# Half of the gate and up rows of two feed-forward layers by seven block products for eight, with the sums of weight tiles made by accumulating DMAs

## The chip, the cores and the metric

The program runs on one core of one Trainium2 chip. The metric is the device time of one execution in microseconds (us). Engines are named as the profile names them: PE multiplies matrices, PEld loads its stationary operands, DVE and ACT do elementwise work, POOL is the fourth engine and can issue DMAs, SP issues DMAs. PSUM holds the results of PE in eight banks of 128 x 512 numbers.

## What is computed

A decoder trunk of two layers on 256 tokens of 2048 features, in float32: a state-space layer (S5) with a gated output, then an attention layer, each followed by the same feed-forward part. Only that part is touched:

```python
def rmsnorm(x, g):
    xf = x.astype(jnp.float32)
    y = xf * lax.rsqrt(jnp.mean(xf * xf, axis=-1, keepdims=True) + EPS)
    return (y * g.astype(jnp.float32)).astype(x.dtype)

def swiglu(u, w_gate, w_up, w_down):
    return (jax.nn.silu(u @ w_gate) * (u @ w_up)) @ w_down
...
        u = rmsnorm(h, g_ffn[i])
        h = h + swiglu(u, w_gate[i], w_up[i], w_down[i])
```

Here u is 256 x 2048, w_gate and w_up are 2048 x 5632, w_down is 5632 x 2048.

## The kernel before

Every weight matrix is cut on the host into tiles of 512 rows by 512 columns, 1 MB each, and 344 such tiles pass through one stream of **jobs** (`jobs`, `add`). A job loads its tile into a raw buffer (`load_upto`, SP's queue, a ring of three), splits it into a high and a low part in two halves of 1024 elements a partition (`split_upto`: `hi` by ACT on line 98, `lo` = raw - hi by DVE on line 99), and multiplies (`mm3`, lines 108 to 110): for each of four row blocks of 128 and each half of the tokens three products of 128 x 128 by 128 x 512, high by high, low by high and high by low, so 24 matmuls a job. The activations stand split in the same way (`uT`, from `hT_blocks`, lines 141 to 146).

The gate and up work of a layer is cut into 11 **chunks** of 512 columns, chunks 0 to 5 and then 6 to 10, each part followed by its share of the down products. A chunk is eight jobs: gate with row groups 0 to 3, then up with row groups 0 to 3. Behind them come `gate_evac` (Silu, line 686, ACT), `up_evac` (times up, line 693, DVE) and `g_rows` (for each token half four transposes on PE, line 701, the high part on ACT, line 704, the low part on DVE, line 705).

The order is written out by hand. `run_stream` emits for job i: its own split if that isn't done, its matmuls, the split of job i+1, and then the functions hung on job i (`after`, filled from `pend`). Every engine takes its instructions in this order. So an evacuation that hangs on job i stands on ACT and DVE behind the split of job i+1 and ahead of the split of job i+2, which is wanted when job i+2 starts. `hi` and `lo` are two buffers each; the split of a job needs the buffers of the job two before it.

```python
            j.mm(j)
            split_upto(i + 2)
            for f in j.after:
                f()
```

## Time and profile before

| | us |
|---|---|
| median of 3 runs (2116.31 to 2117.63) | 2116.36 |
| profiled execution, its own time | 2113.61 |
| its span, first to last instruction | 2111.8 |
| PE busy | 2082.5 (99%) |
| DVE busy | 1135.2 (54%) |
| ACT busy | 905.6 (43%) |
| POOL busy | 150.1 (7%) |

The sums are made against the profiled execution: 2113.61, of which 1.8 us lie around the span. A busy share is an average over the whole program, so the stretch that is changed has to be looked at by itself. The granted clock of PE is 0.998 of full speed over the span.

### The profile page before, as it was taken

To read this page: it belongs to the slowest core of one execution; us is meant where nothing else is said; L and a number is where in the kernel's file an instruction comes from. 1 tells how busy PE (TensorE), PEld (TensorE's weight loads), DVE (VectorE), ACT (ScalarE), POOL (GpSimd) and SP (SyncE) were. 2 spreads that over 40 slices of the span, in tenths; PEclk is the share of its full clock that TensorE was granted. 3 is DMA by queue.
4 is the path that set the end of the run, shared out by engine and by line. 5 is a ranking of instruction groups with operands and counts; after the bars stand their busy time and mean duration, and the time that the engine had idled before them with its cause. 6 is when DMAs were issued, how large, how long until landed. Compare 5 with 4: busy or idle time off the path is not lost.

```text
span 2111.8 us, 27975 instructions
## 1 busy us (share of the span) xinstructions
PE 2082.5 (99%) x11712; PEld 1754.9 (83%) x11712; DVE 1135.2 (54%) x1661; ACT 905.6 (43%) x1161; POOL 150.1 (7%) x105
## 2 busy tenths in 40 slices
...
GB/s 140 25 126 157 197 190 188 197 183 197 182 197 199 181 197 180 198 180 180 180 160 180 172 167 160 181 193 184 185 194 193 186 199 190 189 192 186 195 194 149
DMA packets 54046, 376.14 MB, mean 178 GB/s; under 512 B 6432, under 2 KB 6944, under 8 KB 9120
## 3 DMA queue, kind: packets, MB, share of 16 engines
...
q14 instruction: 35, 0.29, 0.0%
...
## 4 chain that ended last, share of the span: by engine, by line
PE 95%; DVE 3%; ACT 1%; issue 1%; DMA 0%; SPq 0%; ACTq 0%; POOLq 0%; POOL 0%
PE acc L109 18%; PE acc L110 18%; PE acc L108 18%; PE x L110 4%; PE x L108 4%; PE x L109 4%; PE tr L109 4%; PE tr L108 4%; PE tr L110 4%; PE acc L793 3%; PE acc L792 3%; PE acc L791 3%; PE x L464 1%; PE tr L141 1%; PE acc L273 1%
## 5 line engine op out<-in xcount | busy, mean ns | idle before, releaser
L99 DVE TENSOR_TENSOR lo<-raw,hi 128x1024 fp32r<-128x1024 f32 x674 | 805.9, 1237 | 674.5 <-ACT hi L98 674.4
L98 ACT ACTIVATE hi<-raw 128x1024 fp32r<-128x1024 f32 x688 | 690.4, 1052 | 715.4 <-PE acc L109 413.3
L108 PE MATMUL acc<-hi,g 128*128 128x512 f32 x704 | 274.9, 390 | 0.0
L110 PE MATMUL acc<-lo,g 128*128 128x512 f32 x704 | 274.0, 389 | 0.0
L109 PE MATMUL acc<-hi,g 128*128 128x512 f32 x704 | 274.0, 389 | 0.0
L108 PE MATMUL acc<-hi,u_f 128*128 128x512 f32 x640 | 251.1, 392 | 1.1 <-ACT hi L98 1.0
L110 PE MATMUL acc<-lo,u_f 128*128 128x512 f32 x640 | 249.5, 390 | 1.1 <-DVE lo L99 1.1
L109 PE MATMUL acc<-hi,u_f 128*128 128x512 f32 x640 | 249.3, 390 | 0.0
L110 PEld LDWEIGHTS acc<-lo,g 128*128 128x128 f32 x704 | 132.2, 188 | 27.6
L109 PEld LDWEIGHTS acc<-hi,g 128*128 128x128 f32 x704 | 132.2, 188 | 27.1
L108 PEld LDWEIGHTS acc<-hi,g 128*128 128x128 f32 x704 | 132.2, 188 | 27.1
L108 PE MATMUL x<-hi,u_f 128*128 128x512 f32 x384 | 151.3, 394 | 0.0
L110 PE MATMUL x<-lo,u_f 128*128 128x512 f32 x384 | 149.7, 390 | 0.0
L109 PE MATMUL x<-hi,u_f 128*128 128x512 f32 x384 | 149.5, 389 | 0.0
L108 PE MATMUL tr<-hi,u_f 128*128 128x512 f32 x384 | 149.4, 389 | 0.0
L109 PE MATMUL tr<-hi,u_f 128*128 128x512 f32 x384 | 149.4, 389 | 0.0
L110 PE MATMUL tr<-lo,u_f 128*128 128x512 f32 x384 | 149.4, 389 | 0.0
L110 PEld LDWEIGHTS acc<-lo,u_f 128*128 128x128 f32 x640 | 120.1, 188 | 26.9 <-DVE lo L99 1.9
L108 PEld LDWEIGHTS acc<-hi,u_f 128*128 128x128 f32 x640 | 120.2, 188 | 26.4 <-ACT hi L98 1.9
L109 PEld LDWEIGHTS acc<-hi,u_f 128*128 128x128 f32 x640 | 120.2, 188 | 24.8 <-DVE u_f L146 0.3
L110 PEld LDWEIGHTS x<-lo,u_f 128*128 128x128 f32 x384 | 72.1, 188 | 15.2
L108 PEld LDWEIGHTS tr<-hi,u_f 128*128 128x128 f32 x384 | 72.1, 188 | 15.0
...
## 6 DMA issues: line engine op xcount, KB each, us to landing
raw<-w_gate SPq DMA_DIRECT2D x88, 1024.0 KB, 4.8
raw<-w_up SPq DMA_DIRECT2D x88, 1024.0 KB, 4.8
raw<-w_down SPq DMA_DIRECT2D x88, 1024.0 KB, 4.8
raw<-w_kv SPq DMA_DIRECT2D x32, 1024.0 KB, 4.8
raw<-w_glu SPq DMA_DIRECT2D x16, 1024.0 KB, 4.9
raw<-w_q SPq DMA_DIRECT2D x16, 1024.0 KB, 4.8
raw<-w_o SPq DMA_DIRECT2D x16, 1024.0 KB, 4.8
h<-x_tok SPq DMA_DIRECT2D x2, 1024.0 KB, 7.8
```

The costliest lines, as they stand in the source:

```text
L98: act.activation(j.hi[:, s], j.raw[:, s], AF.Copy)
L99: (pool if i < NPRE else dve).tensor_tensor(j.lo[:, s], j.raw[:, s], j.hi[:, s], op=OP.subtract)
L108: pe.matmul(pr, oh, j.hi[:, kb], start=first and kb == 0, stop=False)
L109: pe.matmul(pr, ol, j.hi[:, kb], start=False, stop=False)
L110: pe.matmul(pr, oh, j.lo[:, kb], start=False, stop=last and kb == 3)
L141: pe.transpose(tr[:, bb, a], h[:, a, 128 * b:128 * b + 128], ident)
L273: pe.matmul(wbk[:, 0:w], ident, cs[:, 0:w], start=True, stop=True)
L464: pe.matmul(yb[64 * g2:64 * g2 + 64, g], H[q][r, ri, gl + g2].rearrange("p k c -> p (k c)"), Z[r, :, ri, 2 * (8 * o + g) + b], start=ri == ...
L791: pe.matmul(p, j.hi[:, kb, s], u[:, 0], start=first and kb == 0 and n % 2 == 0, stop=False)
L792: pe.matmul(p, j.hi[:, kb, s], u[:, 1], start=False, stop=False)
L793: pe.matmul(p, j.lo[:, kb, s], u[:, 0], start=False, stop=last and kb == 3 and n % 2 == 1)
```

## The change

In both layers chunk 0 stays as it was in its products. In the other ten chunks of a layer, row groups 2 and 3 stay (four jobs of 24 matmuls), and row groups 0 and 1 are computed together for gate and up by Strassen's method: the activations are a 2 x 2 block matrix (two token halves by two row groups), the weights are one too (two row groups by gate and up), and seven products of blocks stand for eight. Each of the seven is a job of 12 matmuls (`mm1`). Three of them use blocks of `uT`, four use sums of blocks, which `s_combine` makes once a layer (`SC`). It takes the place of `hT_blocks` for eight of the 16 blocks.

The weights of the seven are G0, G1, U1, U0 + G0, U0 + G0 + U1, U1 + U0, and U0 + G0 + U1 + G1 (G and U for gate and up, the digit for the row group). Sums are made in place: after the split of a job that has a successor (`next`), POOL issues a DMA that adds the next 1 MB tile of the weights to the raw buffer. So products 1, 5, 6 and 4 are a chain of three such DMAs, 3 and 7 a chain of one. A chunk has 11 jobs (24, 12, 12, 24, 12, 12, 24, 12, 12, 24, 12 matmuls): plain, 1, 2, plain, 5, 3, plain, 6, 7, plain, 4. `s_evac` puts the products together, with ten DVE instructions of 128 x 512 a chunk where there were two.

`hi` and `lo` are now four tiles for the whole program (`parts`), with no new tile for each job. The raw tiles of the two chains have homes of their own, outside the ring of three.

```diff
+            if j.prev is None:
+                if j.home:
+                    j.raw = big.tile([128, 4, 512], F32, name=f"raw{st['load']}", tag=j.home)
+                else:
+                    j.raw = ring.tile([128, 4, 512], F32, name=f"raw{st['load']}", tag="raw", bufs=3)
+                nc.sync.dma_start(j.raw, j.src[j.t].rearrange("p (k n) -> p k n", k=4))
             st["load"] += 1
...
-            j.hi = ring.tile([128, 4, 512], F32R, name=f"hi{i}", tag="hi")
-            j.lo = ring.tile([128, 4, 512], F32R, name=f"lo{i}", tag="lo")
+            load_upto(i + j.look)
+            if i < 2:
+                parts[i] = [ring.tile([128, 4, 512], F32R, name=f"{nm}{i}", tag=nm) for nm in ("hi", "lo")]
+            j.hi, j.lo = parts[i % 2]
             for p in range(2):
                 s = slice(2 * p, 2 * p + 2)
                 act.activation(j.hi[:, s], j.raw[:, s], AF.Copy)
                 (pool if i < NPRE else dve).tensor_tensor(j.lo[:, s], j.raw[:, s], j.hi[:, s], op=OP.subtract)
+            if j.next is not None:
+                k = j.next
+                k.raw = j.raw
+                pool.dma_start(k.raw, k.src[k.t].rearrange("p (k n) -> p k n", k=4), accum_op=OP.add)
             st["split"] += 1
...
+    def mm1(pr, opnd, j, first, last):
+        for kb in range(4):
+            oh, ol = opnd(0, kb), opnd(1, kb)
+            pe.matmul(pr, oh, j.hi[:, kb], start=first and kb == 0, stop=False)
+            pe.matmul(pr, ol, j.hi[:, kb], start=False, stop=False)
+            pe.matmul(pr, oh, j.lo[:, kb], start=False, stop=last and kb == 3)
...
+    def s_combine(b, un, g):
+
+        if b == 0:
+            SC["t"] = big.tile([128, 2, 4, 4, 128], F32R, name=f"sc_{un}", tag="DA"[un == "u_f1"])
+        tr = bank("tr").rearrange("p (b a t) -> p b a t", b=2, a=2)
+        X = rows.tile([128, 2, 2, 128], F32, name=f"X{b}_{un}", tag="row")
+        V = rows.tile([128, 4, 128], F32, name=f"V{b}_{un}", tag="row")
+        for bb in range(2):
+            for a in range(2):
+                pe.transpose(tr[:, bb, a], h[:, a, 128 * (b + 4 * bb):128 * (b + 4 * bb) + 128], ident)
+        for bb in range(2):
+            k = b + 4 * bb
+            act.activation(X[:, bb], tr[:, bb], AF.Copy, scale=g[:, k:k + 1])
+            act.activation(uT[un][:, 0, k], X[:, bb].rearrange("p a t -> p (a t)"), AF.Copy)
+            dve.tensor_tensor(uT[un][:, 1, k], X[:, bb].rearrange("p a t -> p (a t)"), uT[un][:, 0, k], op=OP.subtract)
+        dve.tensor_tensor(V[:, 2], X[:, 0, 1], X[:, 0, 0], op=OP.subtract)
+        dve.tensor_tensor(V[:, 0], X[:, 0, 1], X[:, 1, 1], op=OP.subtract)
+        dve.tensor_tensor(V[:, 1], X[:, 1, 1], V[:, 2], op=OP.subtract)
+        dve.tensor_tensor(V[:, 3], X[:, 1, 0], V[:, 1], op=OP.subtract)
+        act.activation(SC["t"][:, 0, :, b], V, AF.Copy)
+        dve.tensor_tensor(SC["t"][:, 1, :, b], V, SC["t"][:, 0, :, b], op=OP.subtract)
...
+    for n in range(2):
+        u_pairs(len(jobs) - 2 + n, n, "u_f0", 2)
+    for c in (2, 3):
         u_chunk(len(jobs) - 4 + 2 * c, c, "u_f0", 2)
...
+    def s_opnd(i, un):
+        if i in (1, 2, 4):
+            k0, a = {1: (0, 0), 2: (4, 0), 4: (4, 1)}[i]
+            return lambda part, kb: uT[un][:, part, k0 + kb, 128 * a:128 * a + 128]
+        n = {5: 0, 6: 1, 7: 2, 3: 3}[i]
+        return lambda part, kb: SC["t"][:, part, n, kb]
+
+    def s_job(i, un):
+        o = s_opnd(i, un)
+
+        def f(j):
+            if i in (1, 5, 6, 7):
+                T[i] = bank(T["tags"][{1: 2, 5: 1, 6: 0, 7: 2}[i]])
+                mm1(T[i], o, j, True, True)
+            else:
+                nm, a = {2: ("gate", 0), 3: ("up", 0), 4: ("gate", 1)}[i]
+                mm1(acc[nm][a], o, j, False, i == 4)
+        return f
+
+    def s_evac(n, r):
+        def f():
+            tt = lambda o, x, y, op: dve.tensor_tensor(o, x, y, op=op)
+            if n == 1:
+                T["P"] = row()
+                act.activation(T["P"], T[1], AF.Copy)
+            if n == 7:
+                T["u"] = row()
+                tt(T["u"], T[6], T["P"], OP.subtract)
+            if n == 8:
+                T["v"] = row()
+                tt(T["v"], T[5], T["u"], OP.add)
+                tt(T["P"], acc["gate"][0], T["P"], OP.add)
+                act.activation(T["P"], T["P"], AF.Silu, scale=r[:, 0:1])
+            if n == 9:
+                T["x"] = row()
+                tt(T["x"], T[7], T["v"], OP.add)
+                tt(T["v"], acc["up"][0], T["v"], OP.add)
+                tt(T["v"], T["v"], T["P"], OP.mult)
+            if n == 10:
+                tt(T["u"], T[7], T["u"], OP.add)
+                tt(T["u"], acc["gate"][1], T["u"], OP.subtract)
+                act.activation(T["u"], T["u"], AF.Silu, scale=r[:, 1:2])
+                T["c22"] = acc["up"][1]
+            if n == 11:
+                tt(T["x"], T["c22"], T["x"], OP.add)
+                tt(T["x"], T["x"], T["u"], OP.mult)
...
+                    X = [add(wg, 4 * c + 2, gu_job("gate", un, own, 2, True, False))]
+                    p = {1: add(wg, 4 * c, s_job(1, un), home="EF"[c % 2])}
+                    p[2] = add(wg, 4 * c + 1, s_job(2, un))
+                    X.append(add(wu, 4 * c + 2, gu_job("up", un, own, 2, True, False)))
+                    p[5] = add(wu, 4 * c, s_job(5, un), prev=p[1])
+                    p[3] = add(wu, 4 * c + 1, s_job(3, un), home="W")
+                    X.append(add(wg, 4 * c + 3, gu_job("gate", un, own, 3, False, True, (0,))))
+                    p[6] = add(wu, 4 * c + 1, s_job(6, un), prev=p[5])
+                    p[7] = add(wu, 4 * c, s_job(7, un), prev=p[3])
+                    X.append(add(wu, 4 * c + 3, gu_job("up", un, own, 3, False, True)))
+                    p[4] = add(wg, 4 * c + 1, s_job(4, un), prev=p[6])
+                    for j in jobs[j0:]:
+                        j.look = 4
+                    X[0].pre.append(at_start)
+                    pend.append((j0 + 10, at_end))
+                    for n in (1, 7, 8, 9, 10, 11):
+                        pend.append((j0 + n, s_evac(n, r)))
+                    for a in range(2):
+                        pend.append((j0 + 11 + 2 * a, g_rows(l, hf, c, lambda a=a: T["vx"[a]], lambda a=a: NT[a], a)))
```

On DVE, at the border of two chunks of the first layer, this stands in the kernel before (`lo41` to `lo43` belong to the second, third and fourth job of the new chunk, `row` and `g` to the old one, `g` being the low parts of its transposed rows):

```order
L99 TENSOR_TENSOR lo41_3735<-raw41_3666,hi41_3734 128x1024 x2
L693 TENSOR_TENSOR row145_3606<-acc0_143_3572,row145_3606 128x512
L693 TENSOR_TENSOR row146_3607<-acc2_144_3573,row146_3607 128x512
L99 TENSOR_TENSOR lo42_3769<-raw42_3698,hi42_3768 128x1024 x2
L705 TENSOR_TENSOR g001_3779<-acc1_149_3774,g001_3779 128x4x128
L99 TENSOR_TENSOR lo43_3809<-raw43_3732,hi43_3808 128x1024 x2
L705 TENSOR_TENSOR g001_3779<-acc3_150_3814,g001_3779 128x4x128
```

And this in the changed kernel on DVE at such a border (`raw58` is there the chunk's last sum, product 4; `raw68` the next chunk's first plain job; `raw69` and `raw70` its products 1 and 2):

```order
L108 TENSOR_TENSOR lo1_1496<-raw58_3922,hi1_1495 128x1024 x2
L765 TENSOR_TENSOR row186_4243<-tr_184_4190,row185_4209 128x512
L765 TENSOR_TENSOR row185_4209<-acc0_179_4073,row185_4209 128x512
L765 TENSOR_TENSOR row185_4209<-row185_4209,row177_4046 128x512
L108 TENSOR_TENSOR lo0_1488<-raw68_4182,hi0_1487 128x1024 x2
L765 TENSOR_TENSOR row183_4188<-tr_184_4190,row183_4188 128x512
L765 TENSOR_TENSOR row183_4188<-acc3_174_3988,row183_4188 128x512
L108 TENSOR_TENSOR lo1_1496<-raw69_4203,hi1_1495 128x1024 x2
L765 TENSOR_TENSOR row186_4243<-acc2_180_4074,row186_4243 128x512
L765 TENSOR_TENSOR row186_4243<-row186_4243,row183_4188 128x512
L815 TENSOR_TENSOR g002_4306<-acc1_189_4301,g002_4306 128x4x128
L108 TENSOR_TENSOR lo0_1488<-raw70_4237,hi0_1487 128x1024 x2
```

Between the splits of four jobs that follow each other stand eight evacuating instructions now, three of them ahead of the split of the next chunk's first job.

On POOL, in the same two chunks of the changed kernel, the accumulating DMAs stand in this order (`raw58` and `raw69` are chains of three, `raw62` and `raw73` of one):

```order
L112 DMA raw62_4040<-w_up0 128x2048
L112 DMA raw58_3922<-w_gate0 128x2048
L112 DMA raw69_4203<-w_up0 128x2048 x2
L112 DMA raw73_4322<-w_up0 128x2048
L112 DMA raw69_4203<-w_gate0 128x2048
```

In the kernel before POOL has nothing there.

On DVE, behind the gated output of the first layer, two pairs of blocks of `uT` took this in the kernel before (`hT_blocks`, the first two rows):

```order
L146 SCALAR_TENSOR_TENSOR u_f0_2665<-tr_104_2666,gv_73,u_f0_2665 128x256 x2
L146 SCALAR_TENSOR_TENSOR u_f0_2665<-tr_105_2675,gv_73,u_f0_2665 128x256 x2
L99 TENSOR_TENSOR lo14_2711<-raw14_2603,hi14_2710 128x1024 x2
L596 TENSOR_TENSOR row108_2720<-acc1_102_2623,part2_2048 128x512
L596 TENSOR_TENSOR row109_2721<-acc3_103_2624,part2_2048 128x512
```

and this now (`s_combine`, with `V` the sums of blocks and `sc` their split; the last row is the next pair's):

```order
L185 TENSOR_TENSOR u_f0_2723<-X2_u_f0_2804,u_f0_2723 128x256 x2
L186 TENSOR_TENSOR V2_u_f0_2805<-X2_u_f0_2804 128x128
L187 TENSOR_TENSOR V2_u_f0_2805<-X2_u_f0_2804 128x128
L188 TENSOR_TENSOR V2_u_f0_2805<-X2_u_f0_2804,V2_u_f0_2805 128x128
L189 TENSOR_TENSOR V2_u_f0_2805<-X2_u_f0_2804,V2_u_f0_2805 128x128
L191 TENSOR_TENSOR sc_u_f0_2724<-V2_u_f0_2805,sc_u_f0_2724 128x4x128
L185 TENSOR_TENSOR u_f0_2723<-X3_u_f0_2823,u_f0_2723 128x256 x2
```

Each `x2` on line 146 or 185 is one pair of blocks. To a pair belong five further instructions now, four of them on 128 columns, and the split `lo14` that stood behind the two pairs stands behind two such groups.

## Rows read from the trace of the kernel before

**Rows 1.** Page, parts 1 and 4: busy time by engine, chain of waits by engine

```profile
span 2111.8 us, 27975 instructions
PE 2082.5 (99%) x11712; PEld 1754.9 (83%) x11712; DVE 1135.2 (54%) x1661; ACT 905.6 (43%) x1161; POOL 150.1 (7%) x105
PE 95%; DVE 3%; ACT 1%; issue 1%; DMA 0%; SPq 0%; ACTq 0%; POOLq 0%; POOL 0%
```

**Rows 2.** Windows of gate and up chunks: busy by engine, clock, DMA share, GB/s

```profile
700.00:800.00 100.00, 100.00 (x454) 82.86 (x453) 49.04 (x46) 41.39 (x46) 0.00 (x0) 1.00 0.55 188
```

**Rows 3.** Timeline, ACT, 722 to 740: start, length, line, idle before, releaser

```profile
723.11 2.01 ACT L98 ACTIVATE hi<-raw 128x1024 fp32r<-128x1024 f32 x2 [3.43 <-PE acc L109]
728.55 2.01 ACT L98 ACTIVATE hi<-raw 128x1024 fp32r<-128x1024 f32 x2 [3.43 <-PE acc L109]
```

**Rows 4.** Timeline, DVE, 722 to 742, same columns

```profile
724.20 2.36 DVE L99 TENSOR_TENSOR lo<-raw,hi 128x1024 fp32r<-128x1024 f32 x2 [3.08 <-ACT hi L98]
729.64 2.36 DVE L99 TENSOR_TENSOR lo<-raw,hi 128x1024 fp32r<-128x1024 f32 x2 [3.08 <-ACT hi L98]
```

**Rows 5.** Timeline, PE, around the transposes of a chunk

```profile
700.20 0.39 PE L110 MATMUL acc<-lo,u_f 128*128 128x512 f32 x1
700.43 0.60 PE L701 MATMUL x<-cs,row 128*128 128x128 f32 x4
...
701.57 0.39 PE L108 MATMUL acc<-hi,u_f 128*128 128x512 f32 x1
```

**Rows 6.** Groups by form: line, engine, operation, count, busy us, mean ns

```profile
L99 DVE TENSOR_TENSOR lo<-raw,hi 128x1024 fp32r<-128x1024 f32 x109 | 128.7, 1222 | 126.0 <-ACT hi L98 126.0
...
L98 ACT ACTIVATE hi<-raw 128x1024 fp32r<-128x1024 f32 x108 | 108.5, 1052 | 141.8 <-PE acc L109 78.0 <-PE tr L109 37.7 <-PE x L109 26.1
...
L693 DVE TENSOR_TENSOR row<-acc,row 128x512 f32<-128x512 f32 x20 | 12.8, 681 | 0.0
...
L686 ACT ACTIVATE row<-x,sml 128x512 f32<-128x512 f32 x24 | 14.9, 672 | 0.0
```

**Rows 7.** Timeline, DVE and then ACT, 228 to 236: instructions standing back to back

```profile
230.11 2.36 DVE L99 TENSOR_TENSOR lo<-raw,hi 128x1024 fp32r<-128x1024 f32 x2 [0.47 <-ACT hi L98]
232.39 1.28 DVE L596 TENSOR_TENSOR row<-acc,part 128x512 f32<-128x512 f32 x2
233.59 4.17 DVE L99 TENSOR_TENSOR lo<-raw,hi 128x1024 fp32r<-128x1024 f32 x2
...
229.03 2.00 ACT L98 ACTIVATE hi<-raw 128x1024 fp32r<-128x1024 f32 x2
230.92 0.62 ACT L133 ACTIVATE jk<-h 128x512 f32<-128x512 f32 x1
```

**Rows 8.** Timeline, ACT and then DVE, 1333 to 1340: a `hT_blocks` of four

```profile
1333.92 0.47 ACT L145 ACTIVATE u_f<-tr,gv 128x256 fp32r<-128x256 f32 x1 [0.63 <-PE tr L141]
...
1336.87 0.48 DVE L146 SCALAR_TENSOR_TENSOR u_f<-tr,gv,u_f 128x256 fp32r<-128x256 f32 x1 [0.54 <-ACT u_f L145]
```

**Rows 9.** Windows where `hT_blocks` stands before each feed-forward part; a group of DVE

```profile
232.00:242.00 10.00, 10.00 (x50) 8.36 (x49) 9.46 (x12) 4.62 (x9) 6.17 (x4) 1.00 0.69 236
...
1325.00:1345.00 20.00, 20.00 (x98) 16.72 (x97) 12.46 (x18) 11.96 (x22) 0.00 (x0) 1.00 0.46 159
...
L831 DVE TENSOR_SCALAR row<-row,sm 128x128 f32<-128x128 f32 x16 | 4.6, 287 | 0.6
```

**Rows 10.** DMA issues (count, size, us to landing), and two windows at the start

```profile
raw<-w_gate SPq DMA_DIRECT2D x88, 1024.0 KB, 4.8
...
U<-x_grp SPq DMA_DIRECT2D x2, 1024.0 KB, 15.7
...
5.00:10.00 5.00, 5.00 (x15) 4.10 (x16) 4.70 (x19) 3.55 (x4) 0.00 (x0) 1.00 0.98 398
15.00:20.00 5.00, 2.44 (x14) 1.90 (x12) 4.18 (x8) 2.60 (x3) 4.82 (x5) 1.00 1.02 423
```

**Rows 11.** The shortest group of POOL

```profile
L128 POOL TENSOR_TENSOR sml<-sml,half 128x2 f32<-128x2 f32 x4 | 2.8, 701 | 1122.8 <-DVE sml L127 1122.7
```

79 lines of the change are left out of this document (53 added, 26 removed).

## The prediction

> **What bounds the kernel now.** I read the page first: PE is busy for 99% of the span, and 95% of the chain of waits is PE [rows 1]. Then the windows of the stretch that is changed: among gate and up chunks PE has no gap at all, its clock is granted in full (1.00, the 2.4 GHz level), while DVE is busy for 49 of 100 us, ACT for 41, POOL not at all and the DMA engines for 55% [rows 2]. Then the timelines: a job's split starts on ACT every 5.44 us, when PE lets go of the buffers, and before each DVE has idled 3.08 us [rows 3, 4]. So a job of 24 matmuls costs 5.44 us, a matmul 0.2267, and PE sets the time; whatever is taken off PE is gained until something else is late.
>
> **Products removed.** Each of 20 chunks loses 12 matmuls (four jobs of 24 become seven of 12): 240 x 0.2267 = **-54.4 us**. The transposes stay: four cost (701.57 - 700.20) - 4 x 0.2267 = 0.46 us [rows 5], two groups a chunk. A chunk is 8 x 5.44 + 0.93 = 44.4 us before and 4 x 5.44 + 7 x 2.72 + 0.93 = 41.7 after.
>
> **The splits come closer together.** Eleven jobs are split where eight were. On DVE a pair of halves takes 2.28 us when something stands behind it (232.39 - 230.11), and two evacuations take 1.20 [rows 7], so a chunk's DVE work goes from 8 x 2.28 + 4 x 0.6 = 20.6 of 44.4 us to 11 x 2.28 + 12 x 0.6 = 32.3 of 41.7. That fits on average, but not at the border of two chunks, where eight evacuations stand among four splits. An evacuation that reads the one before it takes its full 0.68 [rows 6] and about 0.05 for the hand-over (from 723.11 + 1.05 on ACT to 724.20 on DVE [rows 3, 4, 6]), so 0.73. I follow DVE through the border, with 0 where PE should start product 4 and 0.2267 a matmul; a job's third matmul is the first to need `lo`, 0.45 behind its start. Before 0, two evacuations, the Silu (0.67) and ACT's half (1.05) [rows 6] leave DVE busy with product 4's split until 0.2. Three dependent evacuations: until 2.3. First half of the plain job's `lo`, 1.22 [rows 6]: ready at 3.5, wanted at 2.72 + 0.45 = 3.17, so PE waits **0.4**. Its second half ends at 4.6; two dependent evacuations: 6.0; the Silu: 6.7; ACT's half of product 1: 7.7; its split on DVE: 10.0; two evacuations: 11.4; the low part of the rows: 12.0; first half for product 2: 13.2. PE, 0.4 late, ends the plain job at 8.56, transposes to 9.03, ends product 1 at 11.75 and wants that half at 12.2: it waits **1.0**. A border costs 1.4 us. There are 16 between Strassen chunks (23 us), four ends of a part with only the first wait (2), and in each layer chunk 7 must wait for accumulators that chunk 6's product 7 holds until the evacuation at 4.6 to 5.2 (2.6 for 1.4, together 2): **+27 us**. If instructions don't overlap (0.68 and 1.22 throughout), the same walk gives 0.8 and 1.4, +40; if DVE enters the border earlier than I think, nothing.
>
> **The sums of activation blocks.** `hT_blocks` works off four blocks in 3.4 us, from 1333.92 to 1337.35 [rows 8]. A pair in `s_combine` takes four ACT steps (4 x 0.4), a low part (0.5, both by lines 145 and 146 [rows 8]), four small dependent instructions on DVE (0.287 each [rows 9] and a hand-over, 1.4) and an ACT copy (0.6), 4.2 us until the next pair can start, and two pairs with the last low part 8.6: 5.2 more, four times in the program. In layer 0 DVE is full there (9.46 of 10 us) and nothing covers it; in layer 1 PE has no gap and DVE is busy for 12.5 of 20 [rows 9], so about 3.1 is covered each time: 2 x 5.2 + 2 x 2.1 = **+14 us**, with 8 to 21 as bounds.
>
> **The accumulating DMAs.** 80 are added. ACT's `hi` of a sum waits for the landing; behind it on ACT and DVE stand the next splits and the evacuations, and PE waits for those. On POOL only the next accumulation stands behind. A chain of three lies in each chunk. Product 1's split is finished at 10.1 in the walk above; three landings, two splits between them (1.05 + 1.13 + 1.22 and hand-overs, 3.5 each) and the first half for product 4 (2.4) make 19.5 + 3 x L, where L is the time from the end of a split to the landing. PE wants it at 43.6 (41.7 + 1.4 + 0.45). So up to **L = 8.0 us** nothing is lost, and each us beyond costs 3 a chunk, 60 in all. Product 7's chain of one has more room.
>
> No row shows an accumulating DMA or a DMA issued by POOL. Below stands a plain load, 4.8 us to landing; above, a load queued behind others, 15.7 [rows 10]. The engines at their fullest move 398 to 423 GB/s [rows 10], 2.55 us for a tile; so of the 4.8, 2.25 are fixed. An accumulation also fetches what it adds to: I add one more pass, 2.55. POOL's shortest instruction is 0.70 [rows 11]: I add that for writing out the transfer. Seven plain loads a chunk hold the same engines for 17.9 of 43 us; an accumulation with 5.1 us of its own meets them for about 1.0. That is **L = 9.0**, nearer to the plain load than to the queued one, and 60 x 1.0 = **+60 us**. If it moves like a plain load, L is about 6.5 and this is 0; at three passes, with the added sharing, L is 11.7 and this is +222.
>
> The row of the plain load prices one pass and says nothing on a second. The Trainium skill (Collectives: The Full Stack, "The bandwidth ceiling: the fold count and why AG ≠ RS ≠ AR") says that a reducing transfer is slow not for the addition but for its two source reads, which share one read queue, with a measured ratio of 1.93 to a copy. By one pass the sum would be a gain of 13 us, by that rule a loss of some 40; no run here shows it yet. The page on DMA: Bandwidth & Descriptors ("Latency and other measured facts") puts the first byte at about 1 us when GpSimd issues and 0.6 from SP, an estimate of 0.4 where I took 0.7, so 18 us less.
>
> SP's queue gains 60 loads (11 tiles a chunk for 8, four of them on POOL); the plain ones are issued a chunk ahead and I cost them at nothing. The second-layer homes of `g` and the four fixed `hi`, `lo` tiles cost nothing either; the latter let a split start at half of the old job, which the walk has in it.
>
> **The sum.** -54.4 + 27 + 14 + 60 = +47 on 2113.6: 2160.6. The median of the runs lies 2.75 above the profiled time, so **2163 us**, slower by 2.2%. About 0.2% (4 us) is what a measurement can tell from no change.
>
> **Rivals.**
> 1. *The accumulations stay hidden, and it ends faster.* A 1 MB accumulation lands within 8.0 us of its split; that is the point from which it decides, at the chain to product 4. For it: 4.8 us for a plain load, and engines 45% idle. Against it: the second pass and POOL. It gives -54.4 + 27 + 14 = -13, so 2103 (2085 to 2118). Chance 0.29, of which 0.24 faster, 0.05 the same.
> 2. *The DMA engines become the bound.* At three passes, 7 x 2.55 + 4 x 7.65 = 48.5 us of transfers a chunk don't fit in 43, and L is over 10.5. For it: 55% are busy already with eight loads [rows 2]. Against it: the plain load's price holds its write as well as its read. With L from 10.5 to 11.7: 2255 to 2325. Chance 0.21.
> 3. *Hidden, but DVE eats the gain.* Without overlap of its instructions the borders cost 40 and the sums 18: +4, so 2120. Chance 0.06, of which 0.03 the same, 0.03 slower.
> 4. *The forecast*, L from 8.2 to 10.5: 2115 to 2255. Chance 0.44, nearly all slower.
>
> The order shows the products and the DMAs as the change describes them, so I keep nothing for a change that doesn't do what it says.
>
> **Range and chances.** 2095 to 2285: below it lies a third of rival 1, above it about half of rival 2. Likeliest case alone: 2115 to 2255. Faster 0.24, the same 0.08, slower 0.68.
>
> **What would show it.** The profile after should have 240 matmuls fewer; DVE at some 75% in chunks; PE waiting for `lo` twice at each border, 0.4 and 1.0 us; and ACT's `hi` waiting for a DMA on POOL's queue three times a chunk. Landings under 8 us would make the forecast wrong downwards, over 10.5 upwards; waits of PE at other places (an accumulator, a plain load that is late) would make it wrong in its reasons.

## The result, and the profile after

The changed kernel takes **2257.2 us** (median of 4 runs, 2256.5 to 2259.0) where the kernel before takes 2116.3 beside it: the ratio is 1.067, with a 95% interval of 1.065 to 1.0687. The sign was forecast, and the time lies in the range, but the loss is 141 us where 47 were reckoned.

The page of the changed kernel: busy time by engine, which answers to [rows 1], the two DMA queues with packets, MB and their share of the 16 engines' span, and DMA issues with count, size and median us to landing, which answer to [rows 10]:

```profile
span 2257.1 us, 28803 instructions
...
PE 2112.9 (94%) x11472; PEld 1737.3 (77%) x11472; DVE 1392.2 (62%) x1981; ACT 1057.9 (47%) x1325; POOL 219.3 (10%) x185
...
q1 hardware_dynamic: 51040, 353.39, 43.3%
q0 software_dynamic: 11520, 83.89, 19.4%
...
raw<-w_gate SPq DMA_DIRECT2D x88, 1024.0 KB, 6.9
...
raw<-w_up SPq DMA_DIRECT2D x68, 1024.0 KB, 6.4
raw<-w_up POOLq DMA_DIRECT2D x60, 1024.0 KB, 10.4
...
raw<-w_gate POOLq DMA_DIRECT2D x20, 1024.0 KB, 9.4
```

PE has its 240 matmuls fewer, but is busy for 94% instead of 99% [rows 1]. The 80 accumulations on POOL's queue (q0) hold the engines for 0.194 x 2257.1 / 80 = 5.5 us each. A plain load lands in 6.9 us where it took 4.8 [rows 10], and in 5.0 again when the accumulations are taken out (below): it now shares the engines. SP's queue has 20 loads fewer, not 60 more as the prediction says (w_up 68 where 88 were); the 80 are POOL's.

One chunk of layer 0, 408 to 462, in the timelines of POOL, ACT and PE (start, length, line, operation, idle time before with its releaser):

```profile
409.81 0.85 POOL L112 DMA_DIRECT2D raw<-w_up  x1 [24.28 <-DVE lo L108]
421.76 0.86 POOL L112 DMA_DIRECT2D raw<-w_up  x1 [11.09 <-DVE lo L108]
424.02 0.86 POOL L112 DMA_DIRECT2D raw<-w_up  x1 [1.41 <-DVE lo L108]
435.94 0.86 POOL L112 DMA_DIRECT2D raw<-w_gate  x1 [11.05 <-DVE lo L108]
461.28 0.86 POOL L112 DMA_DIRECT2D raw<-w_up  x1 [24.48 <-DVE lo L108]
```
```profile
418.00 3.98 ACT L107 ACTIVATE hi<-raw 128x1024 fp32r<-128x1024 f32 x4 [1.73 <-DMA raw<-w_up]
...
432.20 2.00 ACT L107 ACTIVATE hi<-raw 128x1024 fp32r<-128x1024 f32 x2 [7.49 <-DMA raw<-w_up]
439.47 3.90 ACT L107 ACTIVATE hi<-raw 128x1024 fp32r<-128x1024 f32 x4 [5.27 <-DMA raw<-w_up]
```
```profile
431.60 0.39 PE L123 MATMUL x<-lo,u_f 128*128 128x512 f32 x1
433.31 0.50 PE L128 MATMUL acc<-hi,sc_u_f 128*128 128x512 f32 x1 [1.31 <-ACT hi L107]
...
434.57 0.66 PE L130 MATMUL acc<-lo,sc_u_f 128*128 128x512 f32 x1 [0.52 <-DVE lo L108]
435.02 0.63 PE L128 MATMUL acc<-hi,sc_u_f 128*128 128x512 f32 x1
435.45 0.63 PE L129 MATMUL acc<-hi,sc_u_f 128*128 128x512 f32 x1
...
440.58 0.50 PE L128 MATMUL acc<-hi,sc_u_f 128*128 128x512 f32 x1 [1.87 <-ACT hi L107]
```

The sum for product 5 goes out at 409.81 and is there at 418.00. Those for products 6 and 7 go out 2.3 us apart (421.76, 424.02) and land at 432.20 and 439.47. PE waits at the first matmuls of products 6 and 7, and nowhere for product 4, whose sum goes out at 435.94. (The row at 431.60 is the last matmul of the plain job ahead of product 6.) The matmuls between are slow: in product 6 they follow each other every 0.43 us (435.02 to 435.45) instead of 0.2267. A chunk takes 51.5 us, from one accumulation for product 5 to the next (409.81 to 461.28), where 44.4 stood before. The page's 10.4 us for w_up is a median over three products that differ: from issue to landing the median is 8.2 us for product 5, 10.4 for product 6, 14.7 for product 7, and 9.4 for product 4.

Windows of 4 us in this chunk (busy us of PE, PEld, DVE, ACT, POOL; then the granted clock, DMA share, GB/s; before had 1.00, 0.55 and 188 throughout [rows 2]):

```profile
420.00:424.00 4.00, 4.00 (x19) 3.30 (x19) 4.00 (x5) 3.41 (x5) 0.86 (x1) 1.00 1.02 430
...
436.00:440.00 4.00, 2.71 (x8) 1.80 (x6) 0.00 (x0) 0.53 (x1) 0.80 (x1) 0.73 1.00 188
...
444.00:448.00 4.00, 4.00 (x17) 3.16 (x17) 2.99 (x4) 0.98 (x2) 0.00 (x0) 0.88 0.30 63
448.00:452.00 4.00, 4.00 (x19) 3.34 (x18) 3.17 (x4) 3.40 (x4) 0.00 (x0) 1.00 1.01 422
```

With the engines full, plain loads move 422 GB/s (448 to 452). The 188 of 436 to 440 are an accumulation with the end of a plain load beside it, and are less than that although the engines are as full. The granted clock falls from 1.00 to 0.73, towards the 1.2 GHz level, after PE's waits in product 6.

The table is worked out from PE's timeline: a product's loss is the time from its beginning (its wait included) to the next work, less 2.72 us, summed over 20 chunks. The main experiments are in it; what each changed follows.

| kernel | time, us | product 2 | 5 | 6 | 7 | 4 |
|---|---|---|---|---|---|---|
| changed | 2257.2 | 14.5 | 0.5 | 42.5 | 109.9 | 0.3 |
| no accumulations | 2113.7 | 15.3 | 0.3 | 0.0 | 0.0 | 0.3 |
| overwriting, POOL's queue | 2117.3 | 15.2 | 0.2 | 0.0 | 0.4 | 0.3 |
| no product 4's | 2261.6 | 13.1 | 1.2 | 37.8 | 113.9 | 0.3 |
| no product 7's | 2190.9 | 15.2 | 0.6 | 41.5 | 1.1 | 12.7 |
| products 5 and 3 swapped | 2323.6 | 15.0 | 0.0 | 197.2 | 0.9 | 0.3 |
| one home | 2255.6 | 15.4 | 60.4 | 7.4 | 56.4 | 0.3 |
| four plain loads left out | 2185.0 | 14.9 | 0.3 | 4.6 | 57.3 | 0.3 |
| in halves | 2239.1 | 15.1 | 0.2 | 29.5 | 74.9 | 0.3 |
| Silu behind | 2224.5 | 0.5 | 0.3 | 23.7 | 116.2 | 0.3 |
| DVE adds two | 2221.6 | 11.5 | 1.5 | 3.1 | 0.0 | 130.1 |
| DVE adds three | 2154.1 | 15.4 | 1.5 | 2.7 | 0.0 | 28.0 |
| DVE adds three, Silu behind | 2098.6 | 0.7 | 0.3 | 1.8 | 0.0 | 0.4 |

### The profile page after: what moved, and what is told of

Same layout as the page of the kernel before. It is cut to its first block, busy times and chain, and to the rows that moved or that the text cites. A ratio compares the mean times of both kernels' runs of the same rounds, so it can differ in the third digit from the quotient of the medians.

```text
span 2257.1 us, 28803 instructions
## 1 busy us (share of the span) xinstructions
PE 2112.9 (94%) x11472; PEld 1737.3 (77%) x11472; DVE 1392.2 (62%) x1981; ACT 1057.9 (47%) x1325; POOL 219.3 (10%) x185
## 3 DMA queue, kind: packets, MB, share of 16 engines
q0 software_dynamic: 11520, 83.89, 19.4%
## 5 line engine op out<-in xcount | busy, mean ns | idle before, releaser
L108 DVE TENSOR_TENSOR lo<-raw,hi 128x1024 fp32r<-128x1024 f32 x794 | 951.2, 1234 | 629.0 <-ACT hi L107 621.8
L107 ACT ACTIVATE hi<-raw 128x1024 fp32r<-128x1024 f32 x808 | 819.1, 1053 | 595.3 <-PE acc L122 260.5
L121 PE MATMUL acc<-hi,u_f 128*128 128x512 f32 x384 | 153.3, 399 | 9.8 <-ACT hi L107 5.4
L123 PE MATMUL acc<-lo,u_f 128*128 128x512 f32 x384 | 152.1, 396 | 2.5 <-DVE lo L108 2.5
L122 PE MATMUL acc<-hi,u_f 128*128 128x512 f32 x384 | 151.7, 395 | 0.0
L128 PE MATMUL acc<-hi,sc_u_f 128*128 128x512 f32 x176 | 80.9, 460 | 47.4 <-ACT hi L107 47.3
L121 PEld LDWEIGHTS acc<-hi,u_f 128*128 128x128 f32 x384 | 73.5, 191 | 26.9 <-ACT hi L107 6.3
L130 PE MATMUL acc<-lo,sc_u_f 128*128 128x512 f32 x176 | 81.7, 464 | 6.9 <-DVE lo L108 6.7
L122 PEld LDWEIGHTS acc<-hi,u_f 128*128 128x128 f32 x384 | 73.4, 191 | 15.6 <-DVE u_f L166 0.3
L129 PE MATMUL acc<-hi,sc_u_f 128*128 128x512 f32 x176 | 78.3, 445 | 0.0
L121 PE MATMUL tr<-hi,u_f 128*128 128x512 f32 x192 | 76.2, 397 | 0.0
L123 PE MATMUL x<-lo,u_f 128*128 128x512 f32 x192 | 75.4, 393 | 0.4 <-DVE lo L108 0.4
L123 PE MATMUL tr<-lo,u_f 128*128 128x512 f32 x192 | 75.2, 392 | 0.4 <-DVE lo L108 0.4
## 6 DMA issues: line engine op xcount, KB each, us to landing
raw<-w_up POOLq DMA_DIRECT2D x60, 1024.0 KB, 10.4
```

The costliest lines, as they stand in the source:

```text
L107: act.activation(j.hi[:, s], j.raw[:, s], AF.Copy)
L108: (pool if i < NPRE else dve).tensor_tensor(j.lo[:, s], j.raw[:, s], j.hi[:, s], op=OP.subtract)
L121: pe.matmul(pr, oh, j.hi[:, kb], start=first and kb == 0, stop=False)
L122: pe.matmul(pr, ol, j.hi[:, kb], start=False, stop=False)
L123: pe.matmul(pr, oh, j.lo[:, kb], start=False, stop=last and kb == 3 and a in stops)
L128: pe.matmul(pr, oh, j.hi[:, kb], start=first and kb == 0, stop=False)
```

## The experiments

### What the terms of the sum cost

**No accumulations.** The line that issues them is taken out:

```
-                pool.dma_start(k.raw, ..., accum_op=OP.add)
```

> The 80 accumulating DMAs are left out: products 5, 6, 7 and 4 multiply the tile that their predecessor left, so four of seven products are not those of the method. Everything else stays. Theory: of the 199.7 us that the profile after has above 2111.8 - 54.4, products 6 and 7 hold 152.4 (42.5 and 109.9 above 2.72 us each time, 90.9 of it idle and the rest matmuls at the lower clock), all of it because the accumulations of the two land late. Without them 2257 - 152 = 2105 us, from 2097 to 2115. Rival, borders and products: DVE's evacuations and the denser splits hold the products up themselves; then at least half of the loss stays, 2180 or more. A side point: if the borders of two chunks cost 1.05 us in product 2 as in the trace after, that stays too.

Measured: 2113.7 us, 0.9991 of before (0.9981 to 1.0). So the accumulations cost 2257.2 - 2113.7 = 143.5 us, nearly the 152.4 of products 6 and 7; some 9 come back as waits of the next plain job for DVE (0.6 a chunk). The expected 2105 was 9 too low for that reason. A chunk takes 43.4 us. It also says that with every accumulation free the change gains 2.4 us, not 54.

**The activation sums alone.** Every chunk runs as chunk 0 does:

```
-                if c == 0:
+                if True:
```

> All 22 chunks of a pass through gate and up are made as chunk 0 is, by eight full jobs; no product and no accumulation is left, but the sums of activation blocks are still made (and used by nothing), and the fixed tiles hi and lo and the homes of the second layer stay. Theory: the difference to the kernel before is the sums alone. From the anchors of the two traces they cost 11.4 us in layer 0 and about 6.5 in layer 1, so 2116 + 18 = 2134 us, from 2128 to 2140; the prediction had +14. Rival: the fixed hi and lo tiles or the moved homes cost something too: above 2145.

Measured: 2135.5 us, 1.0092 of before (1.0077 to 1.0107): 19.4 us, by the times beside it; the fixed `hi` and `lo` tiles and the moved homes are in it. Then the borders are what is left of 2113.7, with the 54.4 of the products taken as reckoned: 2113.7 - (2116.1 - 54.4 + 19.4) = 32.6. PE's waits without accumulations come near that: 15.3 at product 2, some 0.6 at the first plain job of 14 chunks, and 2.7 and 4.3 at the two chunks that wait for accumulators.

### The second read

**The same DMAs, overwriting.**

```
-                pool.dma_start(k.raw, ..., accum_op=OP.add)
+                pool.dma_start(k.raw, ...)
```

> The 80 DMAs stay where they are, on POOL's queue with the same waits and sizes, but overwrite the tile instead of adding to it (so four of seven products are not those of the method). Theory, the second read: by the shares of the queues an accumulation holds the 16 engines for 5.4 us per MB and a plain load for 2.8; as plain loads the four of a chunk need 11 us of engines instead of 22, land in 5 to 7 us instead of 9 to 15, and the waits of products 6 and 7 go: 2105 to 2125 us. Rival, the queue: what POOL issues is slow whatever it carries (the writing out of the transfer, the software queue); landings stay near 9 to 10 us and the time above 2190.

Measured: 2117.3 us in one run. The page has them so:

```profile
q0 software_dynamic: 11520, 83.89, 11.2%
...
raw<-w_up POOLq DMA_DIRECT2D x60, 1024.0 KB, 6.3
...
raw<-w_gate POOLq DMA_DIRECT2D x20, 1024.0 KB, 5.8
```

Same queue, same bytes, same waits: 0.112 x 2115.4 / 80 = 3.0 us of the engines a tile instead of 5.5, a ratio of 1.85, and a landing 4 us earlier. The queue isn't slow; accumulating is. The Trainium skill's rule on two source reads (Collectives: The Full Stack, "The bandwidth ceiling: the fold count and why AG ≠ RS ≠ AR") has 1.93 for a reducing transfer, there in a ring of cores; the 1.85 of this trace comes near it. That it is the second read, and not the addition, no run here shows.

### Which landing decides

**Without product 4's accumulation, without product 7's.** One of four is taken out in each:

```
+                if k.mm.i != 4:      # the other kernel: 7
                     pool.dma_start(k.raw, ..., accum_op=OP.add)
...
+        f.i = i
```

> Only the accumulation for product 4, the last link of the chain of three, is left out (20 of 80; product 4 multiplies a sum that lacks one term). Theory: it is issued 3.5 us before product 7's lands, behind it in the same queue, and PE waits 0.3 us for product 4 in all 20 chunks: 2240 to 2258 us, nearly no change. The recorded step of the prediction (product 4 stands at the end of the chain that decides): the loss of 143.5 us goes or shrinks to less than half, 2114 to 2185.

> Only the accumulation for product 7 is left out (20 of 80; product 7 multiplies an unsummed tile). Theory: it is the one that PE waits for, and it shares queue and engines with product 6's; without it product 6's lands in about 8.2 us, as product 5's does now, at 430 where 432 is wanted: 2114 to 2130 us. The recorded step of the prediction (only the chain of three to product 4 decides, product 7's chain of one has room): at most a fourth of the engine time is freed, 2220 to 2257.

Measured: 2261.6 without product 4's, no gain at all (one run; above the range by 3.6). The last link of the chain, on which the prediction had set the loss, cost nothing. Without product 7's 2190.9: 66 us are gone with its waits, but 41.5 stay in product 6 and 12.7 come up in product 4. So the expectation missed: product 6's accumulation, alone in its queue, still took 12.2 us (issued at 416.62, ACT starts at 428.81 in that trace). Three plain loads ran beside it for part of that time, issued at 411.04, 411.42 and 421.04; that they are the reason is shown below, where such loads are left out.

**Products 5 and 3 swapped.**

```
-                    p[5] = add(wu, 4 * c, s_job(5, un), prev=p[1])
                     p[3] = add(wu, 4 * c + 1, s_job(3, un), home="W")
+                    p[5] = add(wu, 4 * c, s_job(5, un), prev=p[1])
```

> Products 5 and 3 change places in each chunk, so that the tile of product 7's sum is split, and its accumulation issued, before product 5's split and not 2.3 us behind it. The same work, the same outputs. In the trace after (chunk at 410 to 462) the accumulation for product 6 is issued at 421.8 and that for 7 at 424.0, they land at 432.2 and 439.5, and PE wants them at 432.0 and 434.7. Theory, two accumulations at a time: moved ahead, product 7's goes out near 416.5 and lands near 425, product 6's behind it near 431, both before they are wanted, and nearly all of the 143.5 us that the accumulations cost goes: 2114 to 2150. Rival, capacity: 7 x 2.8 + 4 x 5.4 = 41.2 us of transfers don't fit into a chunk of 43.4 us with its gaps, whatever their order: 2200 or more. Rival, the recorded step (the chain of three to product 4 decides): no change, 2250 to 2260.

Measured: 2323.6 us, 1.098 of before, a clear miss of mine. In POOL's and ACT's timelines:

```profile
427.61 0.86 POOL L112 DMA_DIRECT2D raw<-w_up  x1 [9.26 <-DVE lo L108]
431.23 0.86 POOL L112 DMA_DIRECT2D raw<-w_up  x1 [2.76 <-DVE lo L108]
```
```profile
446.67 3.90 ACT L107 ACTIVATE hi<-raw 128x1024 fp32r<-128x1024 f32 x4 [14.27 <-DMA raw<-w_up]
```

Product 3's tile could be split only once product 2 had let go of the buffer, so its accumulation went out 3.6 us ahead of the other and not 5. The two still collide, and now the second, 15.4 us from issue to landing, is the one that PE wants first. From the first issue to the second landing it is 19.1 us. By the shares of the queues on the changed kernel's page an accumulation takes 5.5 us of the engines and a plain load 0.433 x 2257.1 / 337 = 2.9, so two accumulations and three plain loads are an estimated 2 x 5.5 + 3 x 2.9 = 19.7.

### Own pace or shared engines

**Four plain loads of a chunk left out, and one home.** The first lets the plain jobs use product 2's tile; the second holds two loads for the next chunk back until product 4's split:

```
+                elif j.x and parts.get("p2"):
+                    j.raw = parts["p2"]
...
```
```
-                    p = {1: add(wg, 4 * c, s_job(1, un), home="EF"[c % 2])}
+                    p = {1: add(wg, 4 * c, s_job(1, un), home="E")}
```

> All 80 accumulations as in the changed kernel, but the loads of the four plain jobs of a chunk are left out (they multiply the tile of product 2), so that three plain loads of seven are left; the outputs are not the reference's. Theory, the engines are shared: 4 x 5.4 + 3 x 2.8 = 30 us of transfers a chunk instead of 41; two accumulations behind one another still take 2 + 10.8 us, so product 7's lands near 435 instead of 439.5, some 2 us late instead of 6: 2130 to 2190 us. Rival, the accumulations' own pace: within 20 us of 2257. Third: without the loads the accumulations are hidden altogether, 2114 to 2125.

> All first tiles of the chains get the same home (E) instead of E and F in turn, so that the load of the next chunk's first product waits until product 4's tile has been split, and the loads behind it on SP's queue with it. The same work, the same outputs. In the trace after, three loads for the next chunk are issued from 416 to 426, 30 us before they are used, in the same stretch as the two accumulations (421.8 to 439.5): 2 x 5.4 + 3 x 2.8 = 19.2 us of transfers, and the engines are full until product 7's has landed; from 444 to 448 they are at 0.30. Theory, the engines are shared: with two of the three loads moved behind product 4's split, product 7's lands near 436 and the loss of 152 us in products 6 and 7 falls by half or more: 2140 to 2200 us. Rival, the accumulations' own pace: two of them behind one another in one queue take 17.7 us whatever stands beside them: 2245 or more. Third: the first product's tile is late now: waits of ACT for a load from w_gate, and 2257 or more.

Measured: 2185.0 with the loads left out, at the upper end of its range. Half of the loss goes (72.2 of 143.5 us); the landing falls from 10.4 and 9.4 to 8.1 and 7.9 us, the accumulation's own pace. The other half stays, although no plain load is issued from the accumulation for product 5 until product 7's has landed. POOL's issues, what ACT waits for, and a window with accumulations alone:

```profile
401.99 0.86 POOL L118 DMA_DIRECT2D raw<-w_up  x1 [23.06 <-DVE lo L114]
413.68 0.86 POOL L118 DMA_DIRECT2D raw<-w_up  x1 [10.84 <-DVE lo L114]
...
449.43 0.86 POOL L118 DMA_DIRECT2D raw<-w_up  x1 [22.82 <-DVE lo L114]
```
```profile
409.94 2.96 ACT L113 ACTIVATE hi<-raw 128x1024 fp32r<-128x1024 f32 x3 [1.49 <-DMA raw<-w_up]
...
422.00 2.01 ACT L113 ACTIVATE hi<-raw 128x1024 fp32r<-128x1024 f32 x2 [5.12 <-DMA raw<-w_up]
427.63 3.90 ACT L113 ACTIVATE hi<-raw 128x1024 fp32r<-128x1024 f32 x4 [3.61 <-DMA raw<-w_up]
```
```profile
417.00:421.00 4.00, 4.00 (x19) 3.34 (x18) 1.14 (x1) 0.00 (x0) 0.00 (x0) 1.00 1.00 207
```

Alone, product 5's sum lands in 8.0 us, and those for products 6 and 7 take 13.9 together (413.68 to 427.63), one behind the other, where 17.7 stood with loads beside them. Accumulations alone move 207 GB/s with the engines full, about half of a plain load's 422.

With one home 2255.6, no gain: outside my range and inside the rival's, so by the time alone the rival would have it. The table shows more: product 7's loss halves (109.9 to 56.4), product 6's falls to 7.4, and product 5's rises from 0.5 to 60.4. The two loads that are held back, and those behind them on SP's queue, now run up to and beside product 5's accumulation:

```profile
418.18 5.81 ACT L107 ACTIVATE hi<-raw 128x1024 fp32r<-128x1024 f32 x6 [5.13 <-DMA raw<-w_up]
...
435.62 3.90 ACT L107 ACTIVATE hi<-raw 128x1024 fp32r<-128x1024 f32 x4 [3.66 <-DMA raw<-w_up]
```

It had been issued at 406.57, so 11.6 us. Loads that are moved take the loss with them: the engines are shared. The two for products 6 and 7, now with no plain load beside them, take 13.7 us (issued from 421.92), as they do with the loads left out.

**In halves.**

```
+                for q in range(2):
+                    kk = slice(2 * q, 2 * q + 2)
+                    pool.dma_start(k.raw[:, kk], ..., accum_op=OP.add)
```

> Each accumulating DMA is issued as two of 512 KB, one for each half of the tile. The same bytes, the same outputs. Theory, full engines: the engine time of a chunk stays 41 us, but a link of the chain shortens, since ACT's first half of the sum waits for the first half only: about 2.5 us for each of products 5 and 6, so product 7's landing moves by 3 to 5 us: 2160 to 2215 us. Rival, the landing of the second of the two is set by the sum of the transfers in that stretch alone: 2235 to 2257. Third, twice as many issues on POOL and twice as many transfers cost more: above 2260.

Measured: 2239.1 us in one run, 18 better: the rival's range. An earlier start gave little here.

### The clock, and what sets the period

**PE kept busy.** Throwaway matmuls before products 6 and 7, first 5 and 9, then 3 and 6:

```
+                if i in (6, 7):
+                    for _ in range(5 if i == 6 else 9):      # then 3 and 6
+                        pe.matmul(T[i][:, 0:256], ident, cs[:, 0:256], start=True, stop=True)
```

> Before products 6 and 7 PE makes 5 and 9 throwaway matmuls of 0.43 us each on constants (2.2 and 3.9 us) into the bank that the product then starts anew, so that it is not idle while it waits. Nothing else changes; the outputs are the same. Theory: product 7's start is set by the landing, and of its 109.9 us loss 67.8 are idle and 42 are its own matmuls at 1.2 instead of 2.4 GHz; with PE busy the clock stays and these 42 come back: 2257 - 42 = 2215 us, from 2200 to 2235. Product 6's slow matmuls give nothing, since product 7 waits behind them anyway. Rival, the transfers alone: the engines set a chunk's period and PE's speed in the wait is without effect: 2250 to 2260. Third possibility: the throwaway matmuls are in the way where the wait is shorter than they are (product 6 in 5 of 20 chunks): up to 20 us more.

> As the run with throwaway matmuls, but 3 before product 6 and 6 before product 7 (1.3 and 2.6 us instead of 2.2 and 3.9, which had filled the waits to the end), so that they end before the tile lands. Theory, a closed loop: from product 7's landing DVE works without a gap through the border of two chunks to product 1's split, and from there three accumulations lead to the next landing; PE is in neither part, so its clock in products 6 and 7 costs nothing: 2248 to 2260 us, with the clock near 0.99. Rival, the clock: the slow matmuls of product 7 (42 us in all) come back: 2205 to 2225.

Measured: 2256.9 and 2255.2 us, no change, with a mean granted clock of 0.995 and 0.993 instead of 0.970: the first against its theory, the second as its theory has it. In the first the matmuls filled the waits to their end, so it told little; the second settles it, since there PE still waits for ACT before product 7 in most chunks. The full clock is back and the time stays, so the slow matmuls, 61 of the 152 us in PE's rows, were no cause.

**Silu behind.** In the changed kernel only the two Silu of a chunk move behind the next split on ACT:

```
-                act.activation(T["P"], T["P"], AF.Silu, scale=r[:, 0:1])      # n == 8
+                act.activation(T["P"], T["P"], AF.Silu, scale=r[:, 0:1])      # n == 9, first
-                act.activation(T["u"], T["u"], AF.Silu, scale=r[:, 1:2])      # n == 10
+                act.activation(T["u"], T["u"], AF.Silu, scale=r[:, 1:2])      # n == 11, first
```

> The changed kernel with its 80 accumulating DMAs, and only the two Silu of a chunk issued one step later, behind the next tile's split on ACT; the outputs are the same. PE waits nowhere at that place for them in products 6 and 7, so by PE's waits alone it would give at most the 0.77 us of product 2. Theory, a closed loop of about 51.2 us: product 7's landing, 21 us of ACT and DVE through the border to product 1's split, then three transfers to the next landing. What shortens the border brings product 1's split forward and the whole period with it, by 1.7 to 3.5 us a chunk: 2185 to 2225 us. Rival, full engines: the transfers of a chunk set the period whatever starts them: 2240 to 2257.

Measured: 2224.5 us, 1.0514 of before (1.0496 to 1.0531), 32.7 below the changed kernel, 1.6 us a chunk, at the upper end of its range. Product 2's wait gives 14 of it; the rest comes although products 6 and 7 still wait for landings. So the 51.5 us are a loop: 8.2 from the issue for product 5 to its landing, 3.8 to the next issue, 17.7 to product 7's landing, and 21.8 of splits and evacuations from there to the next chunk's issue (439.47 to 461.28). What shortens a part of the loop shortens the period. The medians over the 16 borders of two such chunks bear it out: 8.1 + 3.8 + 17.7 + 21.9 = 51.5 in the changed kernel. With the Silu behind the last link is 19.4 and the period 50.0; with the loads left out the third is 13.8, the others are as before, and the period is 47.7. PE's matmuls in products 6 and 7 are in none.

### The sums made elsewhere

**On POOL.** Plain loads into the ring, and POOL adds:

```
-                pool.dma_start(k.raw, ..., accum_op=OP.add)
+                for q in range(2):
+                    kk = slice(2 * q, 2 * q + 2)
+                    pool.tensor_tensor(k.raw[:, kk], k.raw[:, kk], k.term[:, kk], op=OP.add)
...
```

> The 80 accumulating DMAs become plain loads by SP into the ring of raw tiles, and POOL, idle there, adds each to the home tile in two halves. The outputs are those of the method. POOL's subtraction of the same shape took 2.4 us a half before the first chunk, so an add of a tile takes about 4.6 us and lands 4.6 us after the split where the accumulation took 8 to 15; eleven plain loads hold the engines for 31 of 43 us. Theory: no product waits for its tile, and the time is the floor that the run without accumulations showed, 2113.7: from 2110 to 2122 us. Rival, DVE and POOL get in each other's way: DVE's instructions get longer by more than a tenth while POOL adds, the borders grow, and it ends at 2130 or more. Third: the ring of three tiles, now shared by nine loads a chunk, makes a plain load late: 2130 or more, with waits on the DMA of the ring's tiles.

Measured: 2307.6 us, 1.0909 of before; the first rival. (The third is out: ACT waits for no weight tile in that trace, only POOL for its terms.) Groups by form, and two pairs of DVE's splits, the first while POOL adds, the second without:

```profile
L111 DVE TENSOR_TENSOR lo<-raw,hi 128x1024 fp32r<-128x1024 f32 x794 | 1202.5, 1553 | 374.2 <-ACT hi L110 373.1
L117 POOL TENSOR_TENSOR raw<-raw,term 128x1024 f32<-128x1024 f32 x160 | 499.9, 3148 | 877.5 <-DMA term<-w_up 686.2 <-DMA term<-w_gate 96.6 <-DVE lo L111 89.6
```
```profile
448.67 5.50 DVE L111 TENSOR_TENSOR lo<-raw,hi 128x1024 fp32r<-128x1024 f32 x2
...
457.10 2.36 DVE L111 TENSOR_TENSOR lo<-raw,hi 128x1024 fp32r<-128x1024 f32 x2 [1.74 <-ACT hi L110]
```

A pair takes 5.50 us where 2.36 are its own. The Trainium skill says so (SBUF — State Buffer, "Who interferes with whom"): a DVE instruction with two inputs in SBUF contends with a GpSimd instruction that reads SBUF. The trace agrees.

**On DVE.** First the terms of products 6 and 7, then product 4's too, then all four; in all of these the activation sums are made in chunk 0, by POOL from the finished operand, but for one run that leaves them where they were:

```
+            for k in j.adds:
+                k.raw = k.prev.raw
+                for q in range(2):
+                    kk = slice(2 * q, 2 * q + 2)
+                    dve.tensor_tensor(k.raw[:, kk], k.raw[:, kk], k.term[:, kk], op=OP.add)
...
+                    X[2].adds, X[3].adds = [p[6], p[7]], [p[4]]      # with three terms
...
```

> Two changes, the outputs are those of the method. First, the sums for products 6 and 7 are no longer accumulations: their terms are plain loads by SP, and DVE, which has idled 7 us there (426 to 433), adds them to the home tiles in 2 x 2.3 us behind the split of the third plain job; the accumulations for products 5 and 4, for which PE waits 0.5 and 0.3 us in all, stay. Second, the sums of activation blocks are made in chunk 0, where DVE is busy for 49 of 100 us, from the finished operand by POOL, ACT and DVE. Transfers are 9 x 2.8 + 2 x 5.4 = 36 us a chunk. Theory: the loss by accumulations goes (floor 2113.7), DVE's adds fit into its gap, and most of the 19.4 us for the activation sums come back: 2095 to 2112 us, faster than before. Rival, DVE: with 4.6 us more a chunk its splits fall behind PE in the products 6 and 7, some 1 us a chunk and more: 2115 to 2150. Rival, transfers: product 5's accumulation now meets the two more loads and lands late: 2130 or more, with waits of ACT for it.

> As the run in which DVE adds the terms of products 6 and 7, but DVE adds product 4's term as well (behind the split of the fourth plain job, where that run left DVE idle for 8.5 us); only product 5's sum is still an accumulating DMA. Ten plain loads and one accumulation are 33.4 us of transfers a chunk. The outputs are those of the method. In that run product 4 held 130.1 of the loss and products 5, 6 and 7 4.6 together. Theory, each accumulation costs only where its landing is waited for: the 130 go and nothing takes their place, 2221.6 - 130 = 2091 us, from 2087 to 2102, faster than the kernel before. Rival, DVE: 6.9 us of adds a chunk push its splits behind PE, 2105 to 2130. Rival, the chain moves on: now product 5's landing is late, since ten loads stand beside it: above 2130, with ACT waiting for it.

> The same with the sums of activation blocks left where the change had made them (ahead of chunk 0), to tell what their place is worth. Theory: the run with those sums alone cost 19.4 us, and in chunk 0 they are covered by DVE's idle half; so 17 to 20 us above the run with late sums, 2105 to 2118. Rival: the sums have to be paid in either place: within 6 us of it.

> As the run in which DVE adds three of the four terms, but product 5's as well, behind product 2's split, in the middle of the border of two chunks; no accumulating DMA is left. The outputs are those of the method. DVE then has 32.3 + 9.1 = 41.4 us of work in a chunk of 43.4. Theory, the border has no room: the add of 2.3 us stands before the split of the second plain job, and PE waits for that or for product 5 some 1 to 2.3 us a chunk: 15 to 45 us above the run with three, 2105 to 2140. Rival: DVE's idle time further on takes it up, within 8 us of the run with three.

Measured: 2221.6, 2154.1, 2172.5 and 2169.8 us. The first two missed their ranges, and the other two the ranges in us that rested on them, though not their differences (18.4 and 15.7). With two terms on DVE the loss moved on to product 4's accumulation (12.6 us to landing), which had been free. With three it ended, but 2154 is not 2091, and beyond what the rival on DVE had; product 5's landing, the other rival, holds 1.5 us of it. The border lost 1.4 us before product 4 and 1.7 at the plain job behind it. Making the activation sums late, with POOL's help, is worth 2172.5 - 2154.1 = 18.4 us, nearly the 19.4 that they had cost; place and engine changed together. The last accumulation on DVE costs 15.7 more.

**DVE adds three, Silu behind.** The edit of the two Silu, shown above, in the kernel with three terms:

> As the run with three terms added by DVE and late activation sums (2154.1), with one edit more: each of the two Silu of a chunk is issued one step later, behind the next tile's split on ACT instead of ahead of it. Nothing else moves; the outputs are those of the method. In that run PE lost 1.2 to 1.7 us at product 4, 1.7 at the first plain job of the next chunk and 1.05 at product 2, and DVE idled 1.74 us twice at the border because ACT's half of a split stood behind a Silu that itself waited for DVE. Theory, the border is ACT and DVE waiting for one another in a fixed order: the two idle pieces go, product 4 doesn't wait, the plain job waits some 0.9 and product 2 nearly not: 2 to 3 us a chunk, 2095 to 2115 us, as fast as the kernel before or faster. Rival, DVE's load alone: 39 us of work in a chunk of 46 leave the border as it is, within 10 us of 2154.

Measured: **2098.6 us, 0.9926 of before (0.9913 to 0.994)**, 0.7% faster than the kernel before and in its range. ACT and then DVE at the border, first without the edit:

```profile
436.73 0.73 ACT L808 ACTIVATE row<-row,sml 128x512 f32<-128x512 f32 x1 [5.37 <-DVE row L788]
437.36 1.99 ACT L110 ACTIVATE hi<-raw 128x1024 fp32r<-128x1024 f32 x2
```
```profile
436.00 0.69 DVE L788 TENSOR_TENSOR row<-x,row 128x512 f32<-128x512 f32 x1
438.44 2.36 DVE L111 TENSOR_TENSOR lo<-raw,hi 128x1024 fp32r<-128x1024 f32 x2 [1.74 <-ACT hi L110]
```

and the same place with it:

```profile
425.02 0.69 DVE L788 TENSOR_TENSOR row<-x,row 128x512 f32<-128x512 f32 x1
425.63 2.35 DVE L111 TENSOR_TENSOR lo<-raw,hi 128x1024 fp32r<-128x1024 f32 x2
```

ACT's half of product 1's split stood behind a Silu that waited for DVE, and DVE then idled 1.74 us for ACT. Now it goes on at once, and a chunk takes 43.1 us where 46 stood. The first plain job still loses some 1.3 us a chunk.

## Why the prediction was right or wrong

The sum of the measured terms: -54.4 (products), +19.4 (activation sums), +32.6 (borders), +143.5 (accumulations) = +141.1, against -54.4, +14, +27, +60.

1. **What bounds.** Right for the kernel before, and the 240 matmuls are gone from the page; their 54.4 us are taken as reckoned, no run measures them by themselves. In the changed kernel the loop of landings and splits sets the time, not PE.
2. **Borders.** Right in kind and nearly in size. Reckoned 0.4 for the first plain job and 1.0 for product 2; without accumulations they lose 0.6 and 1.1. The two chunks that must wait for accumulators lose 2.7 and 4.3, where 2 in all were put down. That the wait of product 2 can be had for nothing (14.5 to 0.5 with the Silu behind) I didn't see: I took the order of ACT's and DVE's instructions as given.
3. **Activation sums.** 19.4 within the bounds of 8 to 21, and nearly all of it comes back when they are made in chunk 0.
4. **Accumulations: the term that failed**, 143.5 for 60. Their price was right: 2 x 2.55 = 5.1 us of the engines were put down, 5.5 measured, and three passes (rival 2) were not seen; POOL's issue takes 0.86 for 0.70. Alone, one lands in 8.0 us, the very limit of the chain to product 4. Two other steps failed:
   - The first is the sentence that product 7's chain of one has more room: only the chain to product 4 was walked. That one waits 0.3 us in all, and taking its last link out changes nothing. Product 7's accumulation waits for DVE to split product 3's tile, 2.3 us behind product 5's, and so runs into product 6's. PE would be through with product 6 at 431.60 + 0.23 + 2.72 = 434.55 if nothing were late, and ACT's half takes 1.1, so product 7's tile is wanted some 24 us behind the issue for product 5; the links take 8.2 + 3.8 + 17.7 = 29.7.
   - The second is the sharing, put down as 1.0 us from an average over the chunk; even that average, 17.9 of 43 us, gives 5.1 x 17.9 / 43 = 2.1, and the 1.0 has no working. The plain loads themselves were put at nothing. Those for the next chunk are issued as buffers come free, here in the same 18 us as both accumulations, and the engines are at 0.30 afterwards; the share of 0.55 over 100 us hid that [rows 2].

   That (10.4 - 8.0) x 60, the page's median landing in the recorded formula, gives 144 is chance: the formula is that of the chain to product 4.
5. **The rivals.** Rival 2's range (2255 to 2325) holds the time that came, not by three passes, but by full engines in one stretch. That the time lies in the range of 2095 to 2285 is owed to that rival's share of it, and is luck as far as the forecast's own mechanism goes. Rival 1's 2103 fell with the late landings; without any accumulation it is 2113.7, between rival 1 and rival 3 (2120).
6. **What would show it.** DVE, said to be at 75% in chunks, is busy for 37.6 of the 56 us of windows in the chunk shown, 67%, since the chunk is longer. PE's two waits for `lo` at a border are there without accumulations (0.6 and 1.1); in the changed kernel the landings mostly hide the first, and the second stays. ACT's `hi` waits for POOL's queue as said, three times a chunk, but PE pays for two of them, at products 6 and 7: the waits at another place that were to make the forecast wrong in its reasons.

That the engines are shared is shown, by loads left out and loads moved. It is half of the loss. The other half is the two accumulations one behind the other: with no plain load beside them they take 13.9 us, and the loop is then 8.0 + 3.7 + 13.9 + 21.8 = 47.4 us (401.99 to 449.43 in that trace), still more than the 43.4 of a chunk without accumulations. An order that keeps these two apart from each other as well was not run.
